# A down projection with five of eight weight pairs in seven products each, some of them side by side

## The chip, the cores and the metric

The kernel runs on one core of one Trainium2 chip. The metric is the device time of one execution in microseconds (us); a kernel's time is the median of its runs. What a measurement of this kernel can tell from no change is stated in the prediction.

## The reference

One layer of a hybrid decoder trunk over 256 tokens of width 2048, all in float32. A token mixer (four gated branches and an output projection) comes first. The change touches the second half only, a dense MLP with a hidden width of 8192:

```
x = x + rmsnorm(merged @ w_out[l], post_mix_g[l])
h = rmsnorm(x, pre_mlp_g[l])
f = jnp.square(jax.nn.relu(h @ w_up[l])) @ w_down[l]
x = x + rmsnorm(f, post_mlp_g[l])
```

## The kernel before, in words

**Split operands.** Every float32 matrix is held as a high part in a reduced float32 format and a low part that is the rest. A product of two such matrices is three matmuls on PE: high with high, high with low, low with high (L824 to L826 in `eight_sums`). `split` (L101) makes the two parts: ACT casts the high part (L102), DVE subtracts it from the source for the low part (L103).

**Weights.** `w_items` lists all weight tiles in the order in which they are used. `w_emit` (L166) loads one of 1 MB into a `raw` tile (three of them) through SP's queue and splits it in pieces of 1024 columns into `hi` and `lo` tiles, four of each. `w_get` hands the next piece to PE and keeps three more split ahead. So ACT and DVE can be at most four pieces ahead of PE, and a `hi` tile can be written again only when PE has done its last matmul on the piece that was in it.

**The MLP.** The hidden width is worked off in four parts (`q` in 0 to 3) of 16 blocks of 128. In the up stretch of a part PE computes the 16 blocks (`block_tr`, tile `up`), and they are split into `fx`. In the down stretch the part is multiplied with its rows of `w_down` (`eight_sums`, tile `sum`): two halves of 1024 output columns in each of the first three parts; in the last part one half is done that way and the other by a plain product (tile `dn`).

**Eight and seven products.** A half of a down stretch takes the 16 blocks as eight pairs. Two blocks times two token halves times two column halves are a 2x2 block product: eight products. For the pairs named in `SEVEN` a scheme of Strassen's kind does it in seven. It needs sums of the hidden blocks (`keep_sums`, made once per part in the up stretch and kept in `sx`) and sums of the weights, which DVE makes in place in `raw` for every half (`seven`, L153): one subtraction over 2x512 columns (L159) and two over 512 (L162, L163). A pair of eight is two pieces, each with four products. A pair of seven is four pieces: two products on the first, one on the second (only 512 columns wide), two each on the third and fourth. The third piece can be split only after L159, the fourth only after L163:

```
return [(b4[:, 0], first), (b4[:, 1, 1], second), (b4[:, :, 0], None), (b4[:, :, 1], None)]
```

Before, the sevens are pairs 0, 2, 4 and 6, so each is followed by a pair of eight.

**Sums in PSUM.** The eight accumulators of a half are evicted by ACT. In the first part they go into `acc` (L1192), in the second and third into `stage` (L1195), and a DMA of POOL's queue adds them to `acc` (L1196). The accumulators of the seven-scheme, M1, M7, M5 and M6 (0 to 3), are complete with the last seven pair; M2, M4, M3 and M8 (4 to 7) after pair 7. In the last part DVE combines them (`evac_l`).

**Order.** Each engine runs its instructions in one order. A scheduler sets these orders when the program is built, from the order of the code and its own estimate of when things are ready, so a change in one place can move instructions of other engines.

Of the kernel before, what the change touches and what calls it, by code (L numbers as in the profile page):

```python
# [8 lines left out]
F32 = mybir.dt.float32  # L9
F32R = mybir.dt.float32r  # L10
# [5 lines left out]
P = 128  # L16
# [10 lines left out]
PC = 2048  # L27
CONSTS = P + 32 + 6 * 4 + 4 * CW
HC = 1024
NQ = 4  # L30
# [2 lines left out]
QK_SCALE = 192 ** -0.5  # L33
TWO_PI = 6.283185307179586

SEVEN = (0, 2, 4, 6)
SEVEN_G = (1, 3, 5)


# [35 lines left out]
def trunk(ctx: ExitStack, tc: tile.TileContext, t: dict):  # L75
# [16 lines left out]
    def w2(name):  # L92
        return sm.tile([P, 512], F32, tag="w2", name=name, bufs=5)
# [7 lines left out]
    def split(src, hi, lo):  # L101
        a = A.copy(hi, src)  # L102
        return a, V.tensor_tensor(lo, src, hi.bitcast(F32), ALU.subtract)  # L103


    def w_items():
        def plain(src, lo=0, hi=None):
            for i in range(lo, src.shape[0] if hi is None else hi):
                yield src[i], PC, HC
        for k in range(0, KD, 2):  # L110
            yield (t["w_q"][k // 4, :, k % 4 * 512:(k % 4 + 2) * 512],
                   t["w_kv"][0, k // 6, :, k % 6 * 288:(k % 6 + 2) * 288]), HC + 576, "first" if k == 0 else "both"
        for i, n in enumerate((6, 6, 4)):
            yield t["w_kv"][1, i, :, :n * 288], n * 288, n // 2 * 288
        for b in range(4):
            yield from plain(t["w_ca"], b, b + 1)
            yield from plain(t["w_cg"], b, b + 1)
        for n in ("w_uqn", "w_uqr", "w_ukn", "w_uv", "w_sv", "w_su", "w_p"):
            yield from plain(t[n])
        projs = ((3, "attn_proj", 2), (2, "sgu_proj", 1), (0, "pool_proj", 1), (1, "conv_proj", 1))  # L120
        for j in range(4):
            for n, (b, proj, npc) in enumerate(projs):
                if j == 0:
                    yield from plain(t["w_g"][b * 4])
                elif n % 2 == 0:
                    b = min(b, projs[n + 1][0])
                    for p in range(8):
                        yield (t["w_g"][b * 4 + j:b * 4 + j + 5:4, p // 2, :, p % 2 * HC:(p % 2 + 1) * HC]
                               .rearrange("c p n -> p c n"), PC, "seven" if p in SEVEN_G else "eight")
                    for _, proj, npc in projs[n:n + 2]:  # L130
                        yield from plain(t[proj], j * npc, (j + 1) * npc)
                if j == 0:
                    yield from plain(t[proj], 0, npc)
        yield from plain(t["w_out"])
        for q in range(NQ):
            if q == 0:
                yield from plain(t["w_up0"])
                yield from plain(t["w_up"], 0, KQ - 4)
            else:
                yield from plain(t["w_up"], q * KQ - 4, (q + 1) * KQ - 4)  # L140
            for h in range(2 if q < NQ - 1 else 1):
                for p in range(8):
                    yield (t["w_down"].rearrange("(r c g) p n -> r g p c n", c=2, g=4)[
                        q * 2 + h, p // 2, :, :, p % 2 * HC:(p % 2 + 1) * HC], PC, "seven" if p in SEVEN else "eight")
            if q == NQ - 1:
                yield from plain(t["w_down"], q * 16 + 8, (q + 1) * 16)

# [107 lines left out]
    def small(name, n=1):  # L255
        return cst.tile([P, n], F32, name=name)
# [528 lines left out]
    def sums(ue, uo):  # L785

        s = w2("s")
        s1, s3, s_2, s4 = (s[:, o * P:(o + 1) * P] for o in range(4))
        V.tensor_tensor(s1, ue[:, P:], uo[:, P:], ALU.add)
        V.tensor_tensor(s3, ue[:, :P], ue[:, P:], ALU.subtract)  # L790
        V.tensor_tensor(s_2, s1, ue[:, :P], ALU.subtract)
        V.tensor_tensor(s4, uo[:, :P], s_2, ALU.subtract)
        return s
# [187 lines left out]
    for c in range(4):  # L981
        ps = [bank(f"o{i}") for i in range(NT)]
        for k in range(0, KD if c < 3 else 8, 2):
            if c == 0 and k == 12:
# [3 lines left out]
                mp = ctx.enter_context(tc.tile_pool(name="mp", bufs=1))  # L988
                oo = mp.tile([P, NT, D], F32, tag="oo", name="oo")
                og = mp.tile([P, NT, D], F32, tag="og", name="og")  # L990
                xg = mp.tile([P, NT, D], F32, tag="xg", name="xg")
# [105 lines left out]

    def keep_sums(p, ue, uo):
        i = SEVEN.index(p)
        split(sums(ue, uo), sx[:, i, 0], sx[:, i, 1])  # L1100

    def first_hidden(fx):
        u = []
# [6 lines left out]
        for c in range(0, 4, 2):  # L1110
# [4 lines left out]
            split(tp.rearrange("p (e s) -> p e s", e=2), fx[:, c:c + 2, 0], fx[:, c:c + 2, 1])  # L1115
            if c // 2 in SEVEN:
                uc = w2("uc")
# [2 lines left out]
            yield 1  # L1120
        done.add("u0")

    stage = [mp.tile([P, PC], F32, tag="rg", name="stage", bufs=2) for _ in range(2)]
    dr = ctx.enter_context(tc.tile_pool(name="dr", bufs=1, space=bass.MemoryType.DRAM))
    kept = dr.tile([P, NT, D], F32, name="kept")
    xr = mp.tile([P, NT, D], F32, tag="og", name="xr")
    sx = mp.tile([P, len(SEVEN), 2, 512], F32R, tag="xg", name="sx")
    fst = [small(f"fst{i}", 4 + i) for i in range(NT)]
    acc = [None, None]

    def sx_at(i, o):
        return tuple(sx[:, i, a, o * P:(o + 1) * P] for a in range(2))

    def combine(h):

# [24 lines left out]
    for q in range(NQ):  # L1160
        fx = big.tile([P, KQ, 2, S], F32R, tag="B", name="fx")
        if q == 0:
            spawn(first_hidden(fx))
            spawn(second_norm())
        if q == NQ - 1:
            spawn(combine(1))
        ue = None
        for b in range(4 if q == 0 else 0, KQ):
            ps = bank("up")
            block_tr(ps, h2)  # L1170
            u = w1("u")
            join(u, ps)
            V.scalar_tensor_tensor(u, u, 0.0, u, ALU.max, ALU.mult)
            split(u, fx[:, b, 0], fx[:, b, 1])
            if b // 2 in SEVEN:
                if b % 2:
                    keep_sums(b // 2, ue, u)
                ue = u
            if q == NQ - 1 and b == 3:
                spawn(combine(0))  # L1180
        until(lambda: q < NQ - 1 or {("sum", 0), ("sum", 1)} <= done)
        until(lambda: {"u0", "r2"} <= done)
        if q == 0:
            acc[0] = mp.tile([P, 8, 512], F32, tag="oo", name="acc0")
            acc[1] = mp.tile([P, 8, 512], F32, tag="og", name="acc1")

        if q == NQ - 1:
            break

        def evac(h, b, ps):  # L1190
            if q == 0:
                A.copy(acc[h][:, b], ps[b])  # L1192
            else:
                e = stage[b // 4][:, b % 4 * 512:(b % 4 + 1) * 512]
                A.copy(e, ps[b])  # L1195
                G.dma_start(acc[h][:, b], e, accum_op=ALU.add)  # L1196

        for h in range(2):
            eight_sums(fx, sx_at, SEVEN, lambda b, ps, h=h: evac(h, b, ps))
        settle()  # L1200
# [9 lines left out]
    def evac_l(b, ps):  # L1210
# [12 lines left out]
        if b in (M2, M4, M3, M8):  # L1223
            V.tensor_tensor(acc[0][:, b], ps[b], acc[0][:, b], ALU.add)
            square_f(int(b in (M4, M8)), int(b in (M3, M8)))
    eight_sums(fx, sx_at, SEVEN, evac_l)
    G.dma_start(xr, kept)
    ps = [bank(f"dn{i}") for i in range(NT)]
    for k in range(0, KQ, 2):
# [5 lines left out]
        if 2 <= k < 10:  # L1235
            i, c = divmod(k // 2 - 1, 2)
# [44 lines left out]
    e = sum_h(0)  # L1281
# [93 lines left out]
```

## Time and profile before

| | us |
|---|---|
| runs: median (lowest to highest of 3) | 1483.17 (1482.36 to 1483.6) |
| profiled execution, its own time | 1482.84 |
| its span in the trace | 1481.1 |
| PE busy | 1464.9 (99%) |
| DVE busy | 1187.5 (80%) |
| ACT busy | 820.1 (55%) |

The span is the stretch from the first to the last instruction in the trace. PE's matmuls overlap: each is recorded with some 0.39 us, while the next one starts much sooner, so PE's pace is read from the starts of successive matmuls and not from their lengths. The same holds, to a lesser degree, for DVE and ACT. An idle time in brackets at the end of a row is the time in which the engine stood before that instruction, with what ended it.

### The profile page before, as it was taken

How to read it: one execution, taken by the hardware profiler on the slowest of the kernel's cores; microseconds unless marked ns; L12 is line 12 of the kernel's file. 1: busy time of each engine (PE TensorE's matmuls, PEld its weight loads, DVE VectorE, ACT ScalarE, POOL GpSimd, SP SyncE). 2: the span in 40 equal slices, each digit the busy share in tenths (PEclk: the TensorE clock that was granted, in tenths of full speed). 3: DMA queues.
4: the chain of work that ended last, by engine and by line, in shares of the span. 5: the costliest groups of instructions: out<-in, count | busy, mean ns of one | idle time of the engine just before them, and what ended most of it. 6: DMA issues, size and time to landing. Idle time of an engine off the chain costs nothing.

```text
span 1481.1 us, 18880 instructions
## 1 busy us (share of the span) xinstructions
PE 1464.9 (99%) x7204; PEld 1238.3 (84%) x7204; DVE 1187.5 (80%) x1680; ACT 820.1 (55%) x1125; POOL 42.4 (3%) x62
## 2 busy tenths in 40 slices
PE   9999999999999999999999999999999999999997
PEld 8888888888888888888788888888888888788886
DVE  6878788977888888887657888777987778878885
ACT  7655655445554554554445756655565556555552
POOL 0100000000000000000000000000011001100000
PEclk9999999999999999999999999999999999999999
DMA  8555544545655645646755746655589557885572
GB/s 295 211 181 177 179 167 156 196 171 171 226 171 199 226 168 202 224 167 231 280 179 217 266 164 206 227 199 177 192 238 289 184 173 220 245 301 184 185 275 95
DMA packets 62443, 304.16 MB, mean 205 GB/s; under 512 B 5713, under 2 KB 6097, under 8 KB 41873
## 3 DMA queue, kind: packets, MB, share of 16 engines
q1 hardware_dynamic: 55504, 280.54, 53.9%
q0 software_dynamic: 6560, 22.29, 5.6%
q8 instruction: 56, 0.92, 0.2%
q14 instruction: 35, 0.28, 0.1%
q10 hardware_dynamic: 288, 0.14, 0.0%
HBM read 290.36 MB, written 4.19 MB: 199 GB/s over the span
## 4 chain that ended last, share of the span: by engine, by line
PE 94%; DVE 2%; DMA 2%; issue 0%; ACT 0%; POOL 0%; DVEq 0%; ACTq 0%; POOLq 0%
PE up L224 15%; PE sum L825 12%; PE sum L826 12%; PE sum L824 12%; PE up L227 8%; PE yb L213 2%; PE yb L214 2%; PE yb L215 2%; PE zg L213 2%; PE zg L215 2%; PE zg L214 2%; PE o L214 1%; PE o L215 1%; PE o L213 1%; DMA xg<-in_x 1%; PE hd L224 1%
## 5 line engine op out<-in xcount | busy, mean ns | idle before, releaser
L103 DVE TENSOR_TENSOR lo<-raw,hi 128x1024 fp32r<-128x1024 f32 (+2 forms) x626 | 720.3, 1171 | 180.2 <-ACT hi L102 174.2
L102 ACT CAST hi<-raw 128x1024 fp32r<-128x1024 f32 (+2 forms) x626 | 623.7, 1010 | 432.1 <-PE sum L826 98.3
L224 PE MATMUL up<-h,hi 128*128 128x512 f32 x960 | 229.9, 391 | 0.0
L224 PEld LDWEIGHTS up<-h,hi 128*128 128x128 f32 x960 | 176.4, 188 | 34.1
L227 PEld LDWEIGHTS up<-h,lo 128*128 128x128 f32 x960 | 123.1, 191 | 4.7
L227 PE MATMUL up<-h,lo 128*128 128x256 f32 x960 | 124.8, 283 | 0.0
L825 PE MATMUL sum<-lo,hx 128*128 128x512 f32 x312 | 121.4, 389 | 0.0
L826 PE MATMUL sum<-hi,hx 128*128 128x512 f32 x312 | 121.4, 389 | 0.0
L824 PE MATMUL sum<-hi,hx 128*128 128x512 f32 x312 | 121.4, 389 | 0.0
L825 PE MATMUL sum<-lo,fx 128*128 128x512 f32 x308 | 120.0, 390 | 1.2 <-DVE lo L103 1.2
L824 PE MATMUL sum<-hi,fx 128*128 128x512 f32 x308 | 119.9, 389 | 0.0
L826 PE MATMUL sum<-hi,fx 128*128 128x512 f32 x308 | 119.8, 389 | 0.0
L252 ACT COPY jn<-up 128x256 f32<-128x256 f32 x60 | 22.3, 372 | 108.8 <-PE up L224 108.8
L253 DVE TENSOR_TENSOR u<-up,jn 128x256 f32<-128x256 f32 x60 | 25.4, 424 | 60.2 <-ACT jn L252 60.1
L825 PEld LDWEIGHTS sum<-lo,fx 128*128 128x128 f32 x308 | 57.8, 188 | 13.9 <-DVE lo L103 1.9
L825 PEld LDWEIGHTS sum<-lo,hx 128*128 128x128 f32 x312 | 58.6, 188 | 12.2
L824 PEld LDWEIGHTS sum<-hi,hx 128*128 128x128 f32 x312 | 58.6, 188 | 12.2
L826 PEld LDWEIGHTS sum<-hi,hx 128*128 128x128 f32 x312 | 58.6, 188 | 12.1
L824 PEld LDWEIGHTS sum<-hi,fx 128*128 128x128 f32 x308 | 57.8, 188 | 12.5 <-ACT hi L102 0.2
L826 PEld LDWEIGHTS sum<-hi,fx 128*128 128x128 f32 x308 | 57.8, 188 | 11.9
L159 DVE TENSOR_TENSOR raw<-raw 128x1024 f32<-128x1024 f32 x46 | 56.1, 1219 | 0.0
L516 DVE SCALAR_TENSOR_TENSOR cy<-glu,consts,cy 128x253 f32<-128x253 f32 (+15 forms) x120 | 55.6, 465 | 0.6
(438 smaller groups left out, 2436.5 us busy)
## 6 DMA issues: line engine op xcount, KB each, us to landing
raw<-in_w_g SPq DMA_DIRECT2D x64, 1024.0 KB, 5.4
raw<-in_w_up SPq DMA_DIRECT2D x64, 1024.0 KB, 4.9
raw<-in_w_down SPq DMA_DIRECT2D x64, 1024.0 KB, 6.0
raw<-in_w_out SPq DMA_DIRECT2D x16, 1024.0 KB, 5.0
raw<-in_attn_proj SPq DMA_DIRECT2D x8, 1024.0 KB, 4.9
acc<-stage POOLq DMA_DIRECT2D x32, 256.0 KB, 11.8
raw<-in_w_ca SPq DMA_DIRECT2D x4, 1024.0 KB, 5.0
raw<-in_w_cg SPq DMA_DIRECT2D x4, 1024.0 KB, 4.9
```

Source lines behind the costliest of these rows:

```text
L102: a = A.copy(hi, src)
L103: return a, V.tensor_tensor(lo, src, hi.bitcast(F32), ALU.subtract)
L159: V.tensor_tensor(b4[:, :, 0], b4[:, 1], b4[:, :, 0], ALU.subtract)
L213: T.matmul(o, xh, wh, start=first, stop=False)
L214: T.matmul(o, xh, wl, start=False, stop=False)
L215: T.matmul(o, xl, wh, start=False, stop=last)
L224: T.matmul(ps, w[0][:, off:off + P], xs[:, k].rearrange("p a s -> p (a s)"), start=first, stop=last)
L227: T.matmul(ps[:, :S], w[1][:, off:off + P], xs[:, k, 0], start=False, stop=False)
L516: V.scalar_tensor_tensor(y, glu[:, b, :S - w], c, y, ALU.mult, ALU.add)
L824: T.matmul(ps[b], xh, wh, start=first, stop=False)
L825: T.matmul(ps[b], xh, wl, start=False, stop=False)
L826: T.matmul(ps[b], xl, wh, start=False, stop=not left[b])
```

## The change

The first three parts now take five pairs in seven products, pairs 0, 2, 3, 5 and 6; the last part takes four, pairs 0, 2, 3 and 5. Pairs 2 and 3 and pairs 5 and 6 are neighbours. The hidden sums of the fifth pair go to a new tile, `sx4`. It takes the place of the second of two `stage` tiles, so that the accumulators 4 to 7 are now evicted to tiles `e` of the ring `w2` (five tiles, shared with the hidden sums in the up stretch). Line numbers after L35 grow by one, those after L1101 by two and so on, up to five.

```diff
-SEVEN = (0, 2, 4, 6)
+SEVEN = (0, 2, 3, 5, 6)
+SEVEN_L = (0, 2, 3, 5)
...
-                        q * 2 + h, p // 2, :, :, p % 2 * HC:(p % 2 + 1) * HC], PC, "seven" if p in SEVEN else "eight")
+                        q * 2 + h, p // 2, :, :, p % 2 * HC:(p % 2 + 1) * HC], PC, "seven" if p in (SEVEN if q < NQ - 1 else SEVEN_L) else "eight")
...
     def keep_sums(p, ue, uo):
         i = SEVEN.index(p)
-        split(sums(ue, uo), sx[:, i, 0], sx[:, i, 1])
+        s = sx[:, i] if i < 4 else sx4
+        split(sums(ue, uo), s[:, 0], s[:, 1])
...
-    stage = [mp.tile([P, PC], F32, tag="rg", name="stage", bufs=2) for _ in range(2)]
+    stage = mp.tile([P, PC], F32, tag="rg", name="stage", bufs=2)
...
-    sx = mp.tile([P, len(SEVEN), 2, 512], F32R, tag="xg", name="sx")
+    sx = mp.tile([P, 4, 2, 512], F32R, tag="xg", name="sx")
+    sx4 = mp.tile([P, 2, 512], F32R, tag="rg", name="sx4", bufs=2)
...
-    def sx_at(i, o):
-        return tuple(sx[:, i, a, o * P:(o + 1) * P] for a in range(2))
+    def sx_at(i, o, which=SEVEN):
+        i = SEVEN.index(which[i])
+        s = sx[:, i] if i < 4 else sx4
+        return tuple(s[:, a, o * P:(o + 1) * P] for a in range(2))
...
-                e = stage[b // 4][:, b % 4 * 512:(b % 4 + 1) * 512]
+                e = stage[:, b * 512:(b + 1) * 512] if b < 4 else w2("e")
...
-    eight_sums(fx, sx_at, SEVEN, evac_l)
+    eight_sums(fx, lambda i, o: sx_at(i, o, SEVEN_L), SEVEN_L, evac_l)
```

Two places of the order show it. The first is DVE in the first half of the first down stretch, from the third piece of pair 2 on. Numbers tell tiles apart; a `lo` row is the low part of one piece, the three `raw` rows are the weight sums of one seven pair. Before, the rows of pairs 2, 3 and 4:

```order
L103 TENSOR_TENSOR lo_7510<-raw_7476,hi_7509 128x1024
L103 TENSOR_TENSOR lo_7527<-raw_7476,hi_7526 128x1024
L103 TENSOR_TENSOR lo_7539<-raw_7536,hi_7538 128x1024
L103 TENSOR_TENSOR lo_7546<-raw_7536,hi_7545 128x1024
L103 TENSOR_TENSOR lo_7558<-raw_7555,hi_7557 128x1024
L103 TENSOR_TENSOR lo_7569<-raw_7555,hi_7568 128x512
L159 TENSOR_TENSOR raw_7555<-raw_7555 128x2x512
L162 TENSOR_TENSOR raw_7555<-raw_7555 128x512
L163 TENSOR_TENSOR raw_7555<-raw_7555 128x512
```

Now, the rows of pairs 2 and 3:

```order
L104 TENSOR_TENSOR lo_7517<-raw_7483,hi_7516 128x1024
L104 TENSOR_TENSOR lo_7534<-raw_7483,hi_7533 128x1024
L104 TENSOR_TENSOR lo_7546<-raw_7543,hi_7545 128x1024
L104 TENSOR_TENSOR lo_7554<-raw_7543,hi_7553 128x512
L160 TENSOR_TENSOR raw_7543<-raw_7543 128x2x512
L163 TENSOR_TENSOR raw_7543<-raw_7543 128x512
L164 TENSOR_TENSOR raw_7543<-raw_7543 128x512
L104 TENSOR_TENSOR lo_7566<-raw_7543,hi_7565 128x1024
L104 TENSOR_TENSOR lo_7576<-raw_7543,hi_7575 128x1024
```

The two low parts of an eight pair (`raw_7536`) that stood between one seven's pieces and the next one's are gone from this place; the next seven's sums follow at once.

The second place is PE in the same half, on the third and fourth piece of a seven pair; `sum` tiles are the accumulators. Before, pair 2:

```order
L824 MATMUL sum_7468<-hi_7509,sx_6715 128x512
L825 MATMUL sum_7468<-lo_7510,sx_6715 128x512
L826 MATMUL sum_7468<-hi_7509,sx_6715 128x512
L824 MATMUL sum_7472<-hi_7509,sx_6715 128x512
L825 MATMUL sum_7472<-lo_7510,sx_6715 128x512
L826 MATMUL sum_7472<-hi_7509,sx_6715 128x512
L824 MATMUL sum_7483<-hi_7526,fx_6718 128x512
L825 MATMUL sum_7483<-lo_7527,fx_6718 128x512
```

Now, pair 3, the second of two neighbours:

```order
L825 MATMUL sum_7475<-hi_7565,sx_6714 128x512
L825 MATMUL sum_7479<-hi_7565,sx_6714 128x512
L825 MATMUL sum_7490<-hi_7575,fx_6718 128x512
L826 MATMUL sum_7475<-lo_7566,sx_6714 128x512
L827 MATMUL sum_7475<-hi_7565,sx_6714 128x512
L826 MATMUL sum_7479<-lo_7566,sx_6714 128x512
L827 MATMUL sum_7479<-hi_7565,sx_6714 128x512
L825 MATMUL sum_7494<-hi_7575,sx_6714 128x512
L826 MATMUL sum_7490<-lo_7576,fx_6718 128x512
```

In the second of two neighbours the scheduler sets two matmuls on the third piece's high part (`hi_7565`) and one on the fourth's (`hi_7575`) ahead of the first one on a low part. The first of two neighbours and the other sevens keep the order of before.

## Rows read from the trace of the kernel before

**Rows 1.** Page, busy time of PE over the span.
```profile
PE 1464.9 (99%) x7204; PEld 1238.3 (84%) x7204; DVE 1187.5 (80%) x1680; ACT 820.1 (55%) x1125; POOL 42.4 (3%) x62
```

**Rows 2.** Windows, four down stretches: PE, PEld, DVE, ACT, POOL busy (count); clock; DMA.
```profile
871.84:953.65 81.81, 81.81 (x361) 67.58 (x360) 71.30 (x72) 53.67 (x65) 0.00 (x0) 1.00 0.61 210
1042.72:1125.32 82.60, 82.17 (x362) 67.47 (x360) 70.08 (x71) 52.14 (x63) 11.13 (x13) 1.00 0.74 227
1214.38:1297.29 82.91, 82.15 (x361) 67.50 (x360) 70.17 (x71) 52.18 (x63) 11.07 (x13) 1.00 0.74 227
1386.36:1427.26 40.90, 40.90 (x181) 33.80 (x180) 36.93 (x40) 25.58 (x30) 0.56 (x1) 1.00 0.62 213
```

**Rows 3.** Timeline of PE from 882: start, length, engine, line, operation.
```profile
882.06 0.39 PE L824 MATMUL sum<-hi,fx 128*128 128x512 f32 x1
...
884.11 0.39 PE L824 MATMUL sum<-hi,sx 128*128 128x512 f32 x1
```

**Rows 4.** Timeline of DVE, 878 to 900, first part's first half.
```profile
877.14 1.82 DVE L103 TENSOR_TENSOR lo<-raw,hi 128x1024 fp32r<-128x1024 f32 x2
878.87 1.22 DVE L159 TENSOR_TENSOR raw<-raw 128x1024 f32<-128x1024 f32 x1
880.13 0.69 DVE L162 TENSOR_TENSOR raw<-raw 128x512 f32<-128x512 f32 x1
880.86 0.69 DVE L163 TENSOR_TENSOR raw<-raw 128x512 f32<-128x512 f32 x1
881.47 1.22 DVE L103 TENSOR_TENSOR lo<-raw,hi 128x1024 fp32r<-128x1024 f32 x1
883.39 5.46 DVE L103 TENSOR_TENSOR lo<-raw,hi 128x1024 fp32r<-128x1024 f32 x5 [0.71 <-ACT hi L102]
888.77 1.22 DVE L159 TENSOR_TENSOR raw<-raw 128x1024 f32<-128x1024 f32 x1
...
898.99 1.22 DVE L159 TENSOR_TENSOR raw<-raw 128x1024 f32<-128x1024 f32 x1
```

**Rows 5.** Timeline of DVE, 1088 to 1102, two full low parts in a row.
```profile
1098.17 2.36 DVE L103 TENSOR_TENSOR lo<-raw,hi 128x1024 fp32r<-128x1024 f32 x2 [1.70 <-ACT hi L102]
```

**Rows 6.** Timeline of ACT, 878 to 900.
```profile
880.21 1.05 ACT L102 CAST hi<-raw 128x1024 fp32r<-128x1024 f32 x1 [2.76 <-DVE raw L159]
882.31 1.05 ACT L102 CAST hi<-raw 128x1024 fp32r<-128x1024 f32 x1 [1.05 <-PE sum L826]
883.67 3.07 ACT L102 CAST hi<-raw 128x1024 fp32r<-128x1024 f32 x3 [0.31 <-PE sum L826]
```

**Rows 7.** Timeline of ACT, 1088 to 1102, second part's second half.
```profile
1094.16 1.06 ACT L102 CAST hi<-raw 128x1024 fp32r<-128x1024 f32 x1 [0.40 <-DVE raw L163]
1097.09 2.00 ACT L102 CAST hi<-raw 128x1024 fp32r<-128x1024 f32 x2 [1.87 <-DMA raw<-in_w_down]
```

**Rows 8.** Timeline of PE at 1098.
```profile
1098.64 0.39 PE L824 MATMUL sum<-hi,fx 128*128 128x512 f32 x1
1099.45 0.50 PE L825 MATMUL sum<-lo,fx 128*128 128x512 f32 x1 [0.42 <-DVE lo L103]
1099.79 0.39 PE L826 MATMUL sum<-hi,fx 128*128 128x512 f32 x1
```

**Rows 9.** Waits of PE, whole span: us in total, times, longest.
```profile
PE sum L825 <- DVE lo L103: 1.2, 2, 0.8
```

**Rows 10.** Timeline of DVE in an up stretch.
```profile
1159.32 0.42 DVE L253 TENSOR_TENSOR u<-up,jn 128x256 f32<-128x256 f32 x1 [1.75 <-ACT jn L252]
```

**Rows 11.** Page, DMA issues: count, KB each, median us to landing.
```profile
acc<-stage POOLq DMA_DIRECT2D x32, 256.0 KB, 11.8
```

**Rows 12.** Waits in the first down stretch: us in total, times, longest.
```profile
DVE lo L103 <- ACT hi L102: 8.5, 12, 1.0
```

## The prediction

> **What bounds the kernel now.** I read the page first: PE is busy for 1464.9 of 1481.1 us [rows 1], so any gain or loss has to show up as PE time. The profiled execution took 1482.84 us, 1.74 us more than its span and 0.33 us below the median of the runs, 1483.17.
>
> Next I cut out the four stretches in which PE works on `sum` [rows 2]: three parts of two halves (81.81, 82.60 and 82.91 us) and the last part of one half (40.90 us). The first has no PE wait in it: 360 matmuls in 81.81 us are 0.2273 us each. The single steps agree: nine matmuls lie between 882.06 and 884.11 [rows 3]. A product is three matmuls, 0.682 us; a pair of seven products is 4.78 us of PE, a pair of eight 5.46 us. In these stretches DVE is busy for 70 to 71 us of some 82, so it has room on the mean. Whether a pair has room is another question.
>
> Third, DVE's timeline over one seven and one eight pair [rows 4], read as steps from start to start. A full low part takes 1.14: two in a row last 2.36, one alone 1.22 [rows 5]. The low parts of a seven's first two pieces take 1.74 us (877.14 to 878.87; the second, half as wide, is 0.60 of it). The three subtractions take 1.26 (L159), 0.73 (L162) and 0.61 us (L163). A seven pair costs DVE 1.74 + 2.60 + 2 x 1.14 = 6.6 us, an eight pair 2 x 1.14 = 2.3 us. So a seven pair takes DVE 1.8 us longer than PE, and an eight pair gives 3.2 us back. Seven and eight together are 8.9 us of the 10.22 us from 888.77 to 898.99; the rest is waiting for ACT's high part.
>
> Fourth, ACT's timeline shows what ties the engines together [rows 6]. The high part of a seven's third piece starts 0.11 us after L159 has ended (878.87 + 1.22, then 880.21). The fourth's, at 882.31, and the next piece's, at 883.67, start when PE releases one of the four `hi` tiles: DVE and ACT can never be more than four pieces ahead, and behind a seven's last piece they are only as far ahead as that allows.
>
> **The change, term by term.** *Products taken out.* Six halves get one more seven pair: 6 x 3 matmuls x 0.2273 = 4.1 us of PE less. The last part keeps four sevens, so nothing is saved there. The Trainium skill, "TensorE: Matmul & The Clock Gate", section "Wait — 56ns, not 53.3ns?", gives 215.7 ns from start to start for such a matmul, where this trace has 227; by that figure the six products would be an estimated 3.9 us. I take 4.1, the row.
>
> *Sevens side by side.* Pairs 2 and 3, and 5 and 6, are now neighbours, twice in each of six halves; in the last part only 2 and 3 are. That makes 13 places. I lay one out from t = 0, where PE begins the first of the two (882.06 in [rows 3]).
> - PE would pass its four pieces by 4.78, the second pair's first two by 6.83, and two high products of its third piece (the order after the change sets these two ahead) by 7.28. Next in its order stands a matmul on the fourth piece's high part.
> - ACT gets the `hi` tile for the second pair's first piece at 1.61 (883.67 less 882.06) and is done 1.05 later, at 2.66; DVE begins its low part at 2.69 (0.03 later, as 1097.09 + 1.05 and 1098.17 in [rows 7] and [rows 5]). DVE's own queue is no earlier hindrance: it left the last low part of the pair before at 1.33 + 1.14 = 2.47 (883.39 in [rows 4]).
> - From there DVE has only work in a row: low parts to 4.43, L159 from 4.43, L162 from 5.69, L163 from 6.42 to 7.11. The third piece's high part starts at 4.43 + 1.22 + 0.11 = 5.76 and ends at 6.81, just as PE comes to it.
> - The fourth piece's high part must wait for L163, which [rows 7] show at 1094.16, where ACT waited for just that. It runs from 7.22 to 8.27, and PE can start 0.05 us later (as after the low part that ends at 1098.17 + 1.22 in [rows 5] and lets PE go at 1099.45 in [rows 8]), at 8.32, where it would have been at 7.28.
>
> So PE stands for 1.04 us, and a matmul after a wait is followed by a longer step, 0.34 us instead of 0.23 (1099.45 to 1099.79 in [rows 8]): 1.15 us in one place. The eight pair behind it gives the lead back, so the next place starts afresh. Lower bound 0.8: the `hi` tile of the second pair's first piece comes free as soon as DVE is ready for it (2.47 instead of 2.69) and the restart costs nothing. Upper bound 1.35: PE also waits shortly for the third piece, with a restart of 0.11 of its own, and in pair 6 the eviction copy that now lies between two high parts on ACT makes the fourth some 0.1 later. I take 1.15, as all its steps are rows. 13 x 1.15 = 15.0 us (10.4 to 17.6). Behind the waiting matmul on PE stand the other nine of the pair and then the next pair's; nothing else can fill the gap.
>
> *Late weights.* In the second and third parts the accumulating DMAs make `raw` late at one spot of the second half: ACT waits until 1097.09 [rows 7] and PE for a low part at 1098.64 to 1099.45 [rows 8], one of two such PE waits in all [rows 9]. These two stretches are 0.79 and 1.10 us longer than the first [rows 2]. The spot is the start of pair 3. Pair 2 started at 1098.64 - 4.78 = 1093.86, so its neighbour's first high part comes at t = 3.23 instead of 1.61: 1.6 us more wait, twice, less the 1.9 us paid already, +1.3 us. Bounds: -1.9, the transfers come in time, and +2.4, half a us later each.
>
> *The rest, at nothing.* One more pair of hidden sums in each of four up parts (the last computes pair 6's and uses none of them) is four small DVE instructions, a cast and a low part, under 2 us on DVE; DVE idles 1.75 us per block there [rows 10] and is ahead by up to four pieces. Without that cover it would be up to 2 us in each. Four evictions per half go to the ring of five `w2` tiles instead of `stage`: a slot comes up again a half (some 41 us) or ten blocks later, against 11.8 us for the transfer that frees it [rows 11]. If it were late, the copy on ACT would hold the high parts queued behind it, up to one transfer. On POOL the load of the last gain row moves behind all accumulations; its first reader is in the following stage. In the last part the early evictions come one pair sooner, with two eight pairs behind them.
>
> Sum: 1482.84 - 4.1 + 15.0 + 1.3 = 1495.0 for a profiled execution, 1495.4 on the median's footing; I say **1495 us**. Ends of the main case: -4.1 + 10.4 - 1.9 = +4.4, 1487.6; and -4.1 + 17.6 + 2.4 = +15.9, 1499.
>
> **The rivals.** *A, the averages decide, and it is faster.* Five sevens and three eights are 5 x 6.6 + 3 x 2.3 = 39.9 us of DVE against 59 x 0.682 = 40.2 us of PE, so DVE would just fit if its lead carried over the second seven. It decides at the fourth piece of the second pair: the high part would have to be there at 7.28, a us sooner than the chain of rows allows. Then only the products show: 1479. For it: no PE wait in the first part now. Against: four `hi` tiles, and a DVE that already waits on PE's releases. 0.06.
>
> *B, shorter waits that just pay for the products.* Break-even is (4.1 - 1.3)/13 = 0.2 us a place, far below 0.8: 1483. 0.03.
>
> *C, DVE falls behind for good.* DVE waits 8.5 us for high parts in the first part now [rows 12], 4.2 us a half. If those waits stay, a half takes 39.9 + 4.2 = 44.1 us, 3.2 more than now: 6 x 3.2 + 1.1 gives 1503. Against: the waits come from being ahead, and go when DVE is late. 0.05.
>
> *D, the clock falls.* Granted clock is 1.00, the 2.4 GHz level, in all four stretches, the two with PE waits among them [rows 2]. If each of 13 longer waits cost the following eight pair the upper level, 24 matmuls of 0.227 us would take twice that, 13 x 5.46 us: 1566. 0.02. The same page of the Trainium skill, section "A second HAM failure mode: psum-queue depth-cycling", tells of a kernel whose short idles between groups of matmuls made the clock go back and forth; no row here shows it at idles of about a us.
>
> That the change does not do what it says has no chance of its own: the order shows six products fewer.
>
> **Numbers.** Main case 0.84. What a measurement can tell from no change is 0.2%, 3 us: only A lies below that, B and a little of the main case's low edge within. Faster 0.06, same 0.04, slower 0.90. The range runs over the main case's own ends, 1488 to 1500; C, D and A are left out.
>
> **What would show it.** The `sum` stretches of the first three parts grow from some 82 to 84 to 87 us, the last to 42. PE waits of about 0.9 us for ACT's high part appear 13 times, on the first matmul of a fourth piece, with L163 as what ACT waited for. In the second half of parts two and three the wait at pair 3 is longest. The up stretches stay the same length. I am wrong if PE's waits in `sum` stay under 3 us in all, if the waits stand at the low part of first pieces instead, or if a copy to `e` holds ACT.

## The result and the profile after

The changed kernel takes 1495.45 us (median of six runs, 1494.63 to 1497.8); the kernel before, run beside it, 1482.32. The ratio is 1.0088, 95% interval 1.0078 to 1.0098: 13 us slower, where 1495 was forecast. The profiled execution of the change took 1494.63 us, its span is 1492.9, 11.8 more than before.

The page's busy times answer to [rows 1]: 18 matmuls fewer, as the six products make, but PE now stands for 25 us of its span and not for 16.

```profile
PE 1467.9 (98%) x7186; PEld 1233.5 (83%) x7186; DVE 1218.0 (82%) x1730; ACT 830.6 (56%) x1141; POOL 42.7 (3%) x62
```

The windows of the four down stretches (columns as in [rows 2]: length, busy time and count of PE, PEld, DVE, ACT and POOL, clock, DMA):

```profile
871.98:957.48 85.50, 82.40 (x356) 65.84 (x355) 79.03 (x82) 56.07 (x69) 0.00 (x0) 1.00 0.58 195
1046.54:1132.74 86.20, 82.63 (x355) 65.76 (x354) 79.13 (x82) 56.06 (x69) 11.83 (x14) 1.00 0.72 218
1221.81:1307.88 86.07, 82.57 (x355) 65.83 (x354) 79.12 (x82) 56.02 (x69) 11.84 (x14) 1.00 0.71 218
1396.95:1439.05 42.10, 41.39 (x181) 33.63 (x180) 38.61 (x43) 24.20 (x28) 0.55 (x1) 1.00 0.65 237
```

They are 3.69, 3.60, 3.16 and 1.20 us longer, 11.65 in all: nearly the whole of the 11.8. The granted clock is 1.00 throughout. The up stretches between them last 89.06 to 89.07 us, as before.

What makes them longer stands in the waits of PE (total, times, longest) and in one group of the page:

```profile
PE sum L825 <- ACT hi L103: 10.9, 15, 1.0
```
```profile
L825 PE MATMUL sum<-hi,fx 128*128 128x512 f32 x278 | 109.8, 395 | 9.4 <-ACT hi L103 9.4
```

In place of the two waits of [rows 9] there are 15. The `hi,fx` group holds 13 of them, 9.4 us, one on the first matmul of the fourth piece of each second neighbour; the other two, on `hi,sx`, are on the third piece of pair 3 in the second half of parts two and three, where the weights come late (below).

Here is the first place. PE's timeline:

```profile
888.82 0.39 PE L827 MATMUL sum<-hi,sx 128*128 128x512 f32 x1
889.07 0.73 PE L825 MATMUL sum<-hi,sx 128*128 128x512 f32 x2
890.52 0.50 PE L825 MATMUL sum<-hi,fx 128*128 128x512 f32 x1 [0.72 <-ACT hi L103]
890.86 0.40 PE L826 MATMUL sum<-lo,sx 128*128 128x512 f32 x1
```

DVE's, with the second neighbour's three subtractions:

```profile
883.54 3.18 DVE L104 TENSOR_TENSOR lo<-raw,hi 128x1024 fp32r<-128x1024 f32 x3 [0.71 <-ACT hi L103]
886.64 1.22 DVE L160 TENSOR_TENSOR raw<-raw 128x1024 f32<-128x1024 f32 x1
887.89 0.69 DVE L163 TENSOR_TENSOR raw<-raw 128x512 f32<-128x512 f32 x1
888.62 0.69 DVE L164 TENSOR_TENSOR raw<-raw 128x512 f32<-128x512 f32 x1
```

And ACT's, the high parts of the third piece and, behind L164, of the fourth:

```profile
887.97 1.05 ACT L103 CAST hi<-raw 128x1024 fp32r<-128x1024 f32 x1 [2.59 <-DVE raw L160]
889.42 3.89 ACT L103 CAST hi<-raw 128x1024 fp32r<-128x1024 f32 x4 [0.40 <-DVE raw L164]
```

With t = 0 at 882.20 (882.06 of [rows 3], in a stretch that begins 0.14 later) L160 starts at 4.44, L163 at 5.69, L164 at 6.42, the fourth high part at 7.22, and PE goes on at 8.32. The prediction had 4.43, 5.69, 6.42, 7.22 and 8.32.

### The profile page after: what moved, and what is told of

It reads as the page before. It is cut to its first block, busy times and chain, and to the rows that moved or that the text cites. A ratio compares the mean times of both kernels' runs of the same rounds, so it can differ in the third digit from the quotient of the medians.

```text
span 1492.9 us, 18934 instructions
## 1 busy us (share of the span) xinstructions
PE 1467.9 (98%) x7186; PEld 1233.5 (83%) x7186; DVE 1218.0 (82%) x1730; ACT 830.6 (56%) x1141; POOL 42.7 (3%) x62
## 4 chain that ended last, share of the span: by engine, by line
PE 88%; DVE 5%; ACT 2%; DMA 2%; issue 1%; POOL 0%; ACTq 0%; SPq 0%; DVEq 0%; POOLq 0%
PE up L225 15%; PE sum L826 10%; PE sum L827 10%; PE sum L825 10%; PE up L228 8%; DVE lo L104 3%; PE yb L214 2%; PE yb L215 2%; PE yb L216 2%; ACT hi L103 2%; PE zg L216 2%; PE zg L214 2%; PE zg L215 2%; PE o L216 2%; PE o L215 2%; PE o L214 2%
## 5 line engine op out<-in xcount | busy, mean ns | idle before, releaser
L103 ACT CAST hi<-raw 128x1024 fp32r<-128x1024 f32 (+2 forms) x638 | 630.2, 1006 | 434.8 <-DVE raw L160 108.1
L104 DVE TENSOR_TENSOR lo<-raw,hi 128x1024 fp32r<-128x1024 f32 (+2 forms) x638 | 730.4, 1166 | 165.9 <-ACT hi L103 160.0
L825 PE MATMUL sum<-hi,fx 128*128 128x512 f32 x278 | 109.8, 395 | 9.4 <-ACT hi L103 9.4
L826 PE MATMUL sum<-lo,fx 128*128 128x512 f32 x278 | 108.4, 390 | 0.0
L827 PE MATMUL sum<-hi,fx 128*128 128x512 f32 x278 | 108.2, 389 | 0.0
L825 PEld LDWEIGHTS sum<-hi,fx 128*128 128x128 f32 x278 | 52.2, 188 | 25.9 <-ACT hi L103 15.1
L160 DVE TENSOR_TENSOR raw<-raw 128x1024 f32<-128x1024 f32 x52 | 63.4, 1219 | 0.0
L826 PEld LDWEIGHTS sum<-lo,fx 128*128 128x128 f32 x278 | 52.2, 188 | 11.2 <-DVE lo L104 0.2
L827 PEld LDWEIGHTS sum<-hi,fx 128*128 128x128 f32 x278 | 52.2, 188 | 11.0
```

The lines of the kernel that those rows point to most:

```text
L160: V.tensor_tensor(b4[:, :, 0], b4[:, 1], b4[:, :, 0], ALU.subtract)
L825: T.matmul(ps[b], xh, wh, start=first, stop=False)
L826: T.matmul(ps[b], xh, wl, start=False, stop=False)
L827: T.matmul(ps[b], xl, wh, start=False, stop=not left[b])
```

## The experiments

**Is it the neighbours, or the rest of the change?** Two runs take the change's storage and set its pairs.

```diff
-SEVEN = (0, 2, 3, 5, 6)
-SEVEN_L = (0, 2, 3, 5)
+SEVEN = (0, 2, 4, 6)
+SEVEN_L = (0, 2, 4, 6)
```

> The storage of the change (one stage tile, sx4, evictions to the ring w2) with the pairs of before: 0, 2, 4, 6 in all parts. Theory N (neighbours: a seven right behind a seven makes PE wait for the fourth piece): no PE wait at fourth pieces, 1482 us, within 2 of before. Rival S (the new storage costs: copies to e wait for transfers): 1487 to 1495, with ACT waiting at e. Rival L (DVE's load of a fifth seven): same as before, 1482.

Measured: 1482.76 us, ratio to before 0.9997 (0.9988 to 1.0006). PE has only the two waits for late weights:

```profile
PE sum L826 <- DVE lo L104: 1.0, 2, 0.8
```

The ring of `e`, the one `stage` and the moved gain load cost nothing.

```diff
-SEVEN = (0, 2, 3, 5, 6)
-SEVEN_L = (0, 2, 3, 5)
+SEVEN = (0, 2, 3, 6)
+SEVEN_L = (0, 2, 3, 6)
```

> Four sevens in every half, as many as before, but two of them neighbours: pairs 0, 2, 3, 6 in all parts. Products and DVE work are those of before. Theory N: seven waits of some 1.2 us, 8.4 us slower than before, 1490.7 (1489 to 1492). Rival L (load): 1482, no PE wait.

Measured: 1492.98 us, ratio 1.0067 (1.0055 to 1.008). Four sevens as before, so as many products and as much work on DVE, but seven places with neighbours: seven waits on the fourth piece, and two for late weights.

```profile
PE sum L825 <- ACT hi L103: 6.5, 9, 0.8
```

So the loss comes with the place of the sevens and not with their number. It is some 2 us more than expected: the two stretches with late weights are 1.3 and 1.8 us longer than the first (84.15, 85.45, 85.99), where before they were 0.8 and 1.1 longer.

**Is it the chain of subtractions ahead of the fourth piece?** First the 2x512 subtraction is left out for second neighbours.

```diff
-        return [(b4[:, 0], first), (b4[:, 1, 1], second), (b4[:, :, 0], None), (b4[:, :, 1], None)]
+        return [(b4[:, 0], None if second_of_two else first), (b4[:, 1, 1], second), (b4[:, :, 0], None), (b4[:, :, 1], None)]
```

> The change with the subtraction over 2x512 columns (L160) left out for pairs 3 and 6 (the second of two neighbours); the output is not the reference's. Theory N with DVE's chain: the fourth piece's high part is there 1.26 us sooner, at 7.06 instead of 8.32 us after the start of the first neighbour, before PE comes to it at 7.28: no waits, only the six products show, 1477 to 1479. Rival H (the four hi tiles alone set the wait, whatever DVE does): waits of about a us stay, 1493 to 1496.

Measured: 1488.86 us, ratio 1.0038 (1.0024 to 1.0052), a miss by some 10 us: half of the loss stays. DVE's timeline shows why:

```profile
887.23 0.69 DVE L164 TENSOR_TENSOR raw<-raw 128x512 f32<-128x512 f32 x1
887.84 1.22 DVE L104 TENSOR_TENSOR lo<-raw,hi 128x1024 fp32r<-128x1024 f32 x1
888.97 0.69 DVE L165 TENSOR_TENSOR raw<-raw 128x512 f32<-128x512 f32 x1
```

The scheduler, which sets the order by its own estimate, put the third piece's low part between the two subtractions that were left. The 1.26 us taken out were nearly filled again by 1.14, so the run told little. In the next one the subtraction is left out again and the order on DVE is held: `issue_after` sets an instruction behind the one that it names, and `queued` does that for the pieces of two neighbours.

```diff
+            with tc.issue_after(e.ins):
+                chain[:] = [V.tensor_tensor(b4[:, 0, 1], b4[:, 0, 1], b4[:, 1, 1], ALU.subtract).ins]
+        return [(b4[:, 0], None if kind == "second" else first), (b4[:, 1, 1], second), (b4[:, :, 0], None), (b4[:, :, 1], None)]
...
+        with queued(kind):
+            newest[:] = [e.ins for e in split(src, *parts)]
```

> The subtraction of line 160 is left out for the second pair of each two neighbours (so its third piece and what is subtracted from it hold other numbers), and this time DVE's order is held: both narrow low parts, the two remaining subtractions, then the third and the fourth piece's low parts. So the chain to the fourth piece's high part is shorter by 1.26 us and nothing slips into it. The theory (the chain of low parts and subtractions ahead of the fourth piece sets the wait, 8.32 against 7.28 in the prediction's ledger): the high part comes at 7.06, PE does not stand there, and what is left is the products taken out: 1477 to 1481 us, with no or short waits for ACT's high parts in the first part. Rival: four high tiles alone decide, whatever DVE does in between: then the 13 waits of 0.7 us stay, 1493 to 1496 us. Where the shorter chain only takes part of it away, 1485 to 1489 us as in the run without a held order.

Measured: 1483.12 us, ratio 1.0001 (0.9992 to 1.001), 12 us below the change. No wait is left in the first part, nor 13 of anything elsewhere:

```profile
PE sum L836 <- DVE lo L104: 1.4, 2, 0.8
```

So the chain sets the wait, and the four `hi` tiles alone do not. Whether a fifth `hi` tile would take the wait away as well was not tried. The time expected was still some 2 us too low. The first stretch is 81.68 us:

```profile
872.08:953.76 81.68, 81.68 (x355) 65.98 (x354) 75.04 (x78) 56.38 (x69) 0.00 (x0) 1.00 0.61 206
```

The 354 matmuls of 0.2273 are 80.5. At each second neighbour PE now comes just before the third piece's low part, shown as a longer step and not as a wait:

```profile
889.13 0.40 PE L835 MATMUL sum<-hi,sx 128*128 128x512 f32 x1
889.46 0.50 PE L836 MATMUL sum<-lo,sx 128*128 128x512 f32 x1
889.80 0.39 PE L837 MATMUL sum<-hi,sx 128*128 128x512 f32 x1
```

0.33 and 0.34 instead of 0.23 twice are 0.2 us a place. Those and slightly longer steps all through (0.2279) take what the products give: rival B's break-even, reached here with a piece of the work left out.

**Can another engine make that subtraction?** POOL makes it, out of place into a spare tile `t1`; for room the row gains and `stage` are held in halves.

```diff
+        if second_of_two:
+            t1 = spare[0]
+            G.tensor_tensor(t1, b4[:, 1], b4[:, :, 0], ALU.subtract)
...
```

> The change with that subtraction done on POOL for the second of two neighbours, out of place into a spare tile, as soon as the weights are in (DVE's other two stay). Row gains and stage are cut into halves to make room. Theory N: as without it, no waits, 1477 to 1480, if POOL needs under 5 us for it. Rival P (POOL is slow or slows DVE while it works): waits of the old size or more stay, 1490 to 1500.

Measured: 1513.17 us, ratio 1.02 (1.0186 to 1.0214), above the theory's range and the rival's. POOL's group, and one of its 13:

```profile
L181 POOL TENSOR_TENSOR t<-raw 128x1024 f32<-128x1024 f32 x13 | 34.1, 2626 | 487.2 <-DMA raw<-in_w_down 390.1 <-DVE raw L174 81.5 <-DVE raw L177 15.6
```
```profile
926.81 2.70 POOL L181 TENSOR_TENSOR t<-raw 128x1024 f32<-128x1024 f32 x1 [23.75 <-DMA raw<-in_w_down]
```

DVE's timeline beside it:

```profile
926.51 0.69 DVE L177 TENSOR_TENSOR raw<-raw 128x512 f32<-128x512 f32 x1
927.24 2.82 DVE L178 TENSOR_TENSOR raw<-raw 128x512 f32<-128x512 f32 x1
929.98 4.24 DVE L115 TENSOR_TENSOR lo<-raw,hi 128x1024 fp32r<-128x1024 f32 x4
```

The 0.69 us subtraction that meets POOL's takes 2.82, and DVE is free only after POOL is done (926.81 + 2.70). It went so in all 13 places: ten times a subtraction of 0.69 took 2.8 to 2.9 us, three times a low part of 1.22 took 2.5 or 3.5. The work was moved off DVE and DVE stood still for it. The Trainium skill, "SBUF — State Buffer", section "Who interferes with whom", says that a DVE instruction with two inputs in SBUF and a GpSimd instruction that reads SBUF shut each other out; the trace agrees, with these numbers.

**The same work, earlier.** DVE itself makes the subtraction out of place, right behind the low part of the first neighbour's third piece, into a spare tile `wd` (room as above, order held).

```diff
+        if kind == "second":
+            wd = spare[0]
+            chain[:] = [V.tensor_tensor(wd, b4[:, 1], b4[:, :, 0], ALU.subtract).ins]
+            return [(b4[:, 0], None), (b4[:, 1, 1], second), (wd, None), (b4[:, :, 1], None)]
...
```

> The same 2 x 512 subtraction is not left out but made early: DVE writes it into a spare tile of its own right behind the low part of the first neighbour's third piece, one piece ahead of where it was, and the second neighbour's chain then starts without it. The work on DVE is the same, only its place differs. The theory (the order of DVE's work decides, not its amount): the fourth piece's high part comes some 0.9 to 1.2 us sooner than in the change, the waits shrink to 0 to 0.3 us a place, 1478 to 1485 us. Rival (the amount of DVE's work around two neighbours decides): the low parts that now stand behind the early subtraction come late instead, and 13 waits of about the same sum appear on other pieces: 1491 to 1497 us.

Measured: 1489.61 us, ratio 1.0043 (1.003 to 1.0055): 6 us better than the change, 5 worse than expected. The first stretch bears the theory out, with waits of 0.28 in two places in place of 0.7 to 1.0 in four:

```profile
875.21:957.76 82.55, 81.98 (x356) 66.00 (x354) 78.79 (x82) 56.45 (x69) 0.00 (x0) 1.00 0.60 203
1046.82:1130.99 84.17, 82.18 (x355) 66.00 (x354) 78.83 (x82) 56.49 (x69) 11.92 (x14) 1.00 0.74 222
```

The four stretches sum to 292.26 us, 7.6 less than the change's 299.87. Two things keep the time from falling further. In the second and third part the early subtraction (`wd`) waits on DVE for late weights and holds low parts behind it; PE waits 0.93 and 0.61 us there in the second part, 1.00 and 0.61 in the third:

```profile
1100.61 1.23 DVE L186 TENSOR_TENSOR wd<-raw 128x1024 f32<-128x1024 f32 x1 [1.56 <-DMA raw<-in_w_down]
```

And the down projection begins 3.2 us later than in the change: far ahead of it, in the first output stage (`o`), PE stood once, and the clock fell behind that.

```profile
724.17 0.80 PE L247 MATMUL o<-lo,mx 128*128 128x512 f32 x1 [2.40 <-DVE lo L115]
724.77 0.63 PE L248 MATMUL o<-hi,mx 128*128 128x512 f32 x1
725.19 0.63 PE L246 MATMUL o<-hi,mx 128*128 128x512 f32 x1
```

**PE's own order.** In the third and fourth piece of second neighbours the products with the weights' low part come last.

```diff
+                if two:
+                    T.matmul(ps[b], xl, wh, start=False, stop=False)
+                    tail.append((ps[b], xh, wl, not left[b]))
...
+            for o, xh, wl, stop in tail:
+                T.matmul(o, xh, wl, start=False, stop=stop)
```

> Only PE's order changes: in the third and the fourth piece of a second neighbour all products with the high part of the weights come first and those with the low part last, so PE comes to the fourth piece's high part later by two matmuls, 0.45 us, and has other work until then. The theory (PE arrives too early at one high part and nothing else): the wait falls by 0.4 to 0.45 us in each of 13 places, 1489 to 1491 us. Rival (the second neighbour's chain sets a time that PE cannot get round, since the low parts behind it are as late): the wait moves to the low part of the third or the fourth piece and the time stays 1494 to 1497 us.

Measured: 1490.66 us, ratio 1.0049 (1.0035 to 1.0062), as expected. The stretches are 83.75, 85.44, 84.72 and 41.61 us, 4.35 less than the change's together, where 13 x 0.45 would be 5.9: part of the wait moves to the third piece's high part (0.25 us). The profiled execution is the slowest of five, 1493.44, with a 2.2 us idle in that output stage, although its row gains are whole.

**Both together, and another order of pairs.** `early_hi` joins the last two. `order_only` is the change with the second half's pairs in another order, so that places fall from 13 to 9. `order_early_hi` is all three.

```diff
+ORDER = (0, 1, 2, 3, 4, 5, 6, 7), (0, 1, 2, 4, 3, 7, 5, 6), (0, 1, 2, 4, 3, 6, 5, 7)
...
-            for p in range(8):
+            for n, p in enumerate(order):
```

> The two edits that each took part of the wait away are put together: the second neighbour's 2 x 512 subtraction early, into a tile of its own, and in its third and fourth piece the products with the low part of the weights last. With the early subtraction alone the first part's sum stretch was 82.55 us, of which 1.86 us were longer steps behind late pieces of second neighbours (0.28 us waits at the fourth high part, and 0.2 us steps at the third low part); both go if PE comes 0.45 us later to each. Theory (only the time at which PE comes to the two late pieces counts): first stretch 80.6 to 81.2 us, last 40.9 to 41.0, the second and third 83 to 83.6, since the early subtraction there stands before DVE's queue while the weights of pair 3 are still on their way; together 3.5 to 4.5 us less than with the early subtraction alone, 1485 to 1487 us. Rival (the low parts that the early subtraction pushes back are the bound): the stretches stay at 82.5 and 84.2, 1489 to 1490 us.

Measured: 1489.3 us, ratio 1.0039 (1.0026 to 1.0052). The stretches are 82.01, 83.62, 83.62 and 41.08, 1.9 less than with the early subtraction alone, half of what was expected: the stretches lie between the theory's and the rival's. The time stays where the rival had it, and part of that is again the output stage, with an idle of 3.2 us.

> The change with nothing but the order of the pairs changed, in the weights' loading and the products alike: the second half of each of the first three parts takes them as 0, 1, 2, 4, 3, 7, 5, 6, so that its sevens are neighbours only once, at its end, and the last part as 0, 1, 2, 4, 3, 6, 5, 7, with no neighbours. The sevens are as many as in the change, and places fall from 13 to 9. Theory (each place costs 1.2 us and a seven costs nothing else): 4 x 1.2 = 4.8 us less, the last sum stretch 40.9 us again and the first 84.0 to 84.4: 1489.5 to 1491.5 us. Rival (five sevens to three eights are more than DVE can carry however they are placed): the waits move to other pieces of the second half, 1493 to 1496 us.

Measured: 1490.35 us, ratio 1.0052 (1.0039 to 1.0064), as expected: 5.1 us below the change for four places fewer. But the sum agrees better than its parts. The stretches (84.34, 85.64, 85.72 and 40.91) fall by only 3.3 us together: the place at the end of a half costs some 1.4 us, and in parts two and three PE now waits 0.77 and 0.78 us for a low part elsewhere in the second half. The rest lies outside them: the down projection begins 0.85 us earlier than in the change, and the three up stretches last 88.86 to 88.87 us instead of 89.06 to 89.07. The last stretch, where no neighbours are left, is what it was before:

```profile
1393.42:1434.33 40.91, 40.91 (x182) 33.79 (x181) 36.94 (x40) 25.59 (x30) 0.54 (x1) 1.00 0.62 212
```

> All three together: nine places of neighbours, none of them at the spot where the weights come late; there the early subtraction and the products with the low part last. Theory: the products taken out are all that is left in the first part (354 matmuls by 0.2273 us = 80.5; 80.5 to 81.0 us against 81.8 before), the second and third 0.8 to 1.1 us longer as before the change, the last 40.9: 3 to 4 us less than before, 1479 to 1481 us, faster than both kernels. Rival (what the early subtraction displaces shows at the end of the half, or the weights come late at another spot): 1482 to 1486 us, no faster than before.

Measured: 1485.18 us, ratio 1.0015 (1.0006 to 1.0024), some 4 us above the theory and within the rival's range. The stretches are at last below those of before, by 0.56 together, and the loss at the neighbours is gone, no wait in the first:

```profile
877.42:958.58 81.16, 81.16 (x356) 66.14 (x354) 77.14 (x80) 53.59 (x65) 0.00 (x0) 1.00 0.59 196
1047.67:1130.55 82.88, 81.83 (x356) 66.05 (x355) 76.78 (x80) 53.03 (x64) 9.04 (x11) 1.00 0.73 222
```

The second stretch and the third are still 1.72 and 1.55 us longer than the first: the weights come late for pair 3 there, though it is no neighbour now, and PE waits 0.93 and 0.92 us for its low part. And they begin at 877.42 instead of 871.84, most of it from the output stage (an idle of 3.9 us where before has 1.2, and the slower clock behind it), so the version is no faster than before.

**What was lost in the output stage.** A control with nothing but the halved gains and `stage`.

```diff
-        g = mp.tile([P, D], F32, tag="rg", name="rg", bufs=2)
-        G.dma_start(g, t[name].partition_broadcast(P))
-        return g
+        g = [mp.tile([P, D // 2], F32, tag="rg", name="rg", bufs=4) for _ in range(2)]
+        for i in range(2):
+            G.dma_start(g[i], t[name][i * (D // 2):(i + 1) * (D // 2)].partition_broadcast(P))
+        return Halves(g)
...
```

> A control for the three runs with the early subtraction: the change with nothing but the storage that they needed, row gains and stage in two halves of 128 x 1024 each. The gains' loads are four instead of two on POOL's queue, 0.52 us each, ahead of the 2 MB load of the residual input, which those runs issued 1.04 us later and which let DVE and PE stand at the first output stage for 2.4 to 3.9 us (0 to 1.2 us where the gains were whole, in all but one run). Theory (the storage, not the early subtraction, cost those microseconds): the load is issued 2.1 us after the first gain's instead of 1.1, PE idles 2 to 4 us before 726 us, and the time is 2 to 5 us over the change's, 1497.5 to 1500.5 us; the sum stretches stay at 85.5, 86.2, 86.1 and 42.1. Rival (it was chance, or the early subtraction's doing): 1494.5 to 1496.5 us.

Measured: 1498.44 us, ratio 1.0104 (1.009 to 1.0118), in runs from 1495.02 to 1500.67; the profiled one is the fastest, and in its trace PE stands for 1.53 us, less than the 2 to 4 expected. Its stretches are those of the change (85.45, 86.02, 85.97, 42.10). On POOL's queue the load of `xg` (the residual input) stands behind four gain loads; DVE's multiply by a gain waits for it, and low parts of the weights stand behind that on DVE:

```profile
700.26 1.10 POOL L966 DMA_DIRECT2D rg<-in_post_mix_g  x2 [378.95 <-PE tpm L861]
701.34 1.04 POOL L966 DMA_DIRECT2D rg<-in_pre_mlp_g  x2
702.38 0.72 POOL L1007 DMA_DIRECT2D xg<-in_x  x1
```
```profile
720.71 1.29 DVE L1023 TENSOR_TENSOR xg<-xg,rg 128x512 f32<-128x512 f32 x2 [6.37 <-DMA xg<-in_x]
```

Before, the same multiply starts 0.88 us earlier:

```profile
719.83 1.29 DVE L1010 TENSOR_TENSOR xg<-xg,rg 128x512 f32<-128x512 f32 x2 [6.01 <-DMA xg<-in_x]
```

The median is 3.0 us above the change's, but it is one of four runs that lie 5.65 us apart, and the two intervals overlap, so the size of the loss is not settled. That it goes with the halves is shown by the traces together: PE's idle there is 1.5 to 3.9 us in all six with halved gains (the last run below is one), and 0 to 1.2 us in seven of the eight with whole ones. The eighth is the profiled run of PE's own order, with 2.2 us, so the halves are not the only cause. The last run issues that load ahead of the second halves.

```diff
-                pmg = row_gain("post_mix_g")
-                g2 = row_gain("pre_mlp_g")
+                pmg = row_gain("post_mix_g", (0,))
+                g2 = row_gain("pre_mlp_g", (0,))
                 G.dma_start(xg, t["x"].rearrange("(a p) d -> p a d", p=P))
+                gain_load(pmg.tiles, "post_mix_g", (1,))
+                gain_load(g2.tiles, "pre_mlp_g", (1,))
```

> The version with all three edits (order of the pairs, early subtraction, low products last), and the load of the residual input issued behind the first halves of the two gains and ahead of their second halves, which are first read two column groups later. Its sum stretches were 81.16, 82.88, 82.71 and 40.91 us, 0.56 less together than before the change, and 5.5 us were lost at the first output stage. Theory: the stretches stay, the load is issued 1.05 us behind the first gain as before and with half of the gains' bytes ahead of it, PE idles there 0 to 1.2 us: 1481 to 1483 us, no slower than before and 12.5 to 14.5 us below the change. Rival (the accumulating neighbourhood of other transfers makes the load late whatever its place): 1484 to 1487 us as without it.

Measured: 1486.09 us, ratio 1.0019 (1.001 to 1.0028): no gain, a miss. The stretches stay (81.10, 82.72, 82.80, 40.91), and `xg` lands earlier, but the scheduler now puts five gain multiplies between it and the next low parts:

```profile
717.98 0.69 DVE L1059 TENSOR_TENSOR xg<-xg,rg 128x512 f32<-128x512 f32 x1 [6.84 <-DMA xg<-in_x]
...
720.39 0.68 DVE L1058 TENSOR_TENSOR og<-oo,rg 128x512 f32<-128x512 f32 x1
721.00 2.35 DVE L116 TENSOR_TENSOR lo<-raw,hi 128x1024 fp32r<-128x1024 f32 x2
```

PE stands for 3.50 us there. No version ran faster than the kernel before. One with that stage's DVE order held as well was not tried; by the stretches alone it could gain some 0.6 us, less than can be told.

## Why the prediction was right

**Products: as reckoned.** 18 matmuls fewer, 4.1 us. Where the loss at the neighbours is gone (the run with all three edits) the first stretch falls below before's, though by 0.65 us and not by 1.36: five steps of 0.32 to 0.34 us stay at low parts in and behind the neighbours, 0.5 us together, and the other steps are 0.2278 instead of 0.2273.

**Neighbours: right in mechanism and in size.** The ledger's steps hold to 0.01 us in the first place, as shown above. In ten of the 13 places the longer steps around the fourth piece cost 1.11 to 1.14 us, where 1.15 was said. The 0.14 us that PE loses ahead of the third piece (steps of 0.25 and 0.34 from 888.82) were put in the upper bound only. They add nothing: PE goes on at the fourth piece at 8.32 all the same, having waited that much less there. Nor did the eviction copy in pair 6 delay the fourth high part, the other term of that bound. One place, pair 3 in the second half of the first part, costs 1.42 us, above the range's 1.35. There the fourth high part starts 0.39 us after L164's end, where in the other places it is 0.09 to 0.11:

```profile
931.26 0.69 DVE L164 TENSOR_TENSOR raw<-raw 128x512 f32<-128x512 f32 x1
932.34 3.89 ACT L103 CAST hi<-raw 128x1024 fp32r<-128x1024 f32 x4 [0.68 <-DVE raw L164]
```

What held ACT there is not shown. The remaining two places are those with late weights.

**Late weights: the term that was mis-sized.** Predicted was +1.3 us: 1.6 us in each of two places, less the 1.9 paid already. The wait is there, now on the third piece's high part of pair 3:

```profile
1107.25 0.73 PE L825 MATMUL sum<-hi,sx 128*128 128x512 f32 x2 [0.76 <-ACT hi L103]
1108.70 0.50 PE L825 MATMUL sum<-hi,fx 128*128 128x512 f32 x1 [0.72 <-ACT hi L103]
```

ACT's cast behind that load:

```profile
1101.99 1.57 ACT L103 CAST hi<-raw 128x1024 fp32r<-128x1024 f32 x2 [1.33 <-DMA raw<-in_w_down]
```

The step that failed is "Pair 2 started at 1093.86, so its neighbour's first high part comes at t = 3.23". It moves the transfer along with PE. Counted from the stretch's start, the cast came at 54.37 us before and at 55.45 after, 1.1 later; PE, held by the neighbours of the first half, began pair 2 at 51.1 before and at 52.8 after (1099.36), 1.7 later. So the cast comes at t = 2.63 (2.46 in the third part), and from there the ledger holds again: the whole chain, and PE's start on the fourth piece with it, is 1.0 and 0.9 us later than in the other places and not 1.6. These two places cost 2.04 and 1.97 us, together 1.8 more than two others, and the two waits before cost 1.8 by the same steps. The new stalls paid for the old, and the term is nothing instead of +1.3.

In sum, the places come to 14.9 us without the late weights, where 15.0 was said; the late weights to nothing, where 1.3 was said; the products to -4.1. That is 10.8 of the 11.65 us of the stretches. The other 0.8 are in all the other matmuls, which follow each other at some 0.2280 us instead of 0.2273; the prediction has no such term, and what slows them is not shown. So the two misses nearly cancel, and that the forecast came within half a us is in part luck. The other runs of the change lie some 1 us above the profiled one.

**The rivals.** A falls: `one_pair` has the averages of before and still loses 10 us. B is where the run without the subtraction stands. C falls: no further waits grow up in a half, and DVE's 8.5 us of waits for high parts [rows 12] shrink to 4.4. D falls: the clock is 1.00 in all stretches, through idles of up to 1 us; the back and forth that the Trainium skill, "TensorE: Matmul & The Clock Gate", section "A second HAM failure mode: psum-queue depth-cycling", tells of does not show at these.

## What to carry to other kernels

A helper engine that keeps up on the mean can still be late for each of a row of heavy pieces: lay the worst pair of neighbours out against the number of buffers, step by step, and space heavy pieces so that a light one gives the lead back. Before a chain is shortened, look at what the engine's order will put in the gap, and hold the order, or the experiment tests something else. Storage for a spare tile is part of the price: here it put two more DMA issues ahead of a load, and the down projection began 3.2 us later than in the change, against 7.6 us that the early subtraction gained in the stretches.

## What was not expected of the hardware

First, POOL's subtraction stopped DVE's, as shown: a 0.69 us instruction became 2.82.

Second, the clock. PE's windows of the run with the early subtraction, around its 2.40 us idle (PEclk is the third number from the end):

```profile
716.00:724.00 8.00, 5.77 (x26) 4.45 (x24) 2.31 (x3) 3.14 (x3) 0.00 (x0) 1.00 0.58 244
724.00:728.00 4.00, 3.83 (x10) 3.07 (x11) 4.00 (x7) 0.00 (x0) 0.00 (x0) 0.57 0.26 51
728.00:732.00 4.00, 4.00 (x20) 3.26 (x19) 4.00 (x5) 1.80 (x2) 0.00 (x0) 1.00 0.50 211
```

Behind the idle steps are 0.43 us, the 1.2 GHz level, for some 3 us, which adds 1.5 us to the idle. The same shows after 2.2, 3.2, 3.5 and 3.9 us of idle in the other runs. After 1.53 us, in the control with the halves, it does not (nor after 1.58 in the run with POOL):

```profile
723.00:727.00 4.00, 3.81 (x17) 3.12 (x18) 4.00 (x7) 0.94 (x1) 0.00 (x0) 1.00 0.26 55
```
